# Two transformer blocks in split fp32: every split operand at one place modulo 256 bytes, and block 2's depthwise convolution on VectorE alone

## The chip, the cores and the metric

The kernel runs on one core of one Trainium2 chip. The metric is the device time of one execution in microseconds (us). The engines are called PE (TensorE matmul, with PEld for its weight loads), DVE (VectorE), ACT (ScalarE), POOL (GpSimd) and SP (SyncE, which here issues the loads of the weights).

## The reference

Two different transformer blocks follow each other on one sequence of T = 512 positions and width D = 1024, all in fp32. Cut to what matters here:

```python
def first_block(x, mem, ...):
    h = hybrid_mixer(x, w_in, ...)            # gated recurrence and windowed attention
    x = layer_norm(ALPHA * x + h, ...)
    h = memory_cross_attention(x, mem, xa_wq, xa_wkv, xa_wo)
    x = layer_norm(ALPHA * x + h, ...)
    h = (gelu(g) * val) @ ffn_w_down          # g, val: causal_dwconv(x @ ffn_w_up) in halves
    return layer_norm(ALPHA * x + h, ...)

def second_block(x, ...):
    u = rms_norm(x) @ w_in                    # 1024 -> 2560 columns
    y_a = conformer_conv_mixer(u_conf, ...)
    y_b, y_c, y_d = short_conv_mixer(u_sc), moba_attention(u_att), rglru_mixer(u_lru)
    x = x + rms_norm(concat(y_a, y_b, y_c, y_d) @ w_out)
    return x + rms_norm(square(relu(rms_norm(x) @ mlp_w1)) @ mlp_w2)

def conformer_conv_mixer(u, dw_w, dw_b, gn_g, gn_b):
    val, gate = split(u, 2)                   # 256 channels each
    z = val * sigmoid(gate)
    z = causal_depthwise_conv(z, dw_w) + dw_b # 31 taps for each channel
    return silu(group_norm_channels(z, gn_g, gn_b))
```

## The kernel before

**Split products.** Each fp32 operand of a large product is stored as two fp32r tensors: `split` copies it to the high part on ACT (L107) and subtracts that from the source on DVE to get the low part (L108). One product is then three matmuls: high by high, high by low, low by high. In the channel-major form (`cm_phase`, `cm_mm`, `mm3`, L133 to L135) the weight is stationary and 512 positions of the activations stream past it; a *chunk* is 128 output channels, 8 blocks of k, so 24 matmuls of 512 columns. The first five chunks of a phase (the skew) are done in two halves of 256 columns. In the token-major form (`tm_phase`, L218, L219, L222, and `tm_rotate`) the activations are stationary and 512 columns of the weight stream; a *row* is one block of k for all four token tiles, also 24 matmuls. `tm_cols` (L194 to L196) is a token-major form with 256 or 264 columns.

**Where the operands lie.** The split weights rotate through five buffers each of the tags `wh` and `wl` in the pool `wpool`. A buffer has 1056 floats, 4224 bytes in a partition, which is 16.5 times 256. In the built program the buffers of a tag therefore begin alternately at 224 and 96 modulo 256. The activation sets made by `act_set` (x1 to x4, h1 to h3, and the sets of hidden rows hd, hs, md and ms) all begin at 224 modulo 256, and each block of 512 positions in them is a multiple of 256 bytes. The further weight buffers of a phase's last rows (`extra_pool`: wx2 to wx5) begin at 192 (wx2), 224 (wx3), 96 (wx4) and 224 (wx5).

**Order of the work.** The code is written in program order for each engine, and a scheduler interleaves it; each engine then runs its queue in order. Weights come in 1 MB loads on SP's queue into three raw buffers.

**Block 2's mixer.** After the first five chunks of w_in_2, `taps(c)` for each of the two channel halves c puts the convolution's taps in a list `bg` of pending DVE instructions: one tensor_scalar (L1114) and then scalar_tensor_tensor instructions (L1117) of 128x512, that add one tap each into `cacc`. `NPOOL = (6, 20)` taps of the halves go to POOL at once instead, a product (L1121) and an addition (L1123) each, and `conf_mean` later adds POOL's sum `cacp` to `cacc` (L1130). `pump(RATE)` takes 3 instructions off `bg` after each chunk. Behind the taps come the chunks of the attention's queries and keys; `aq_evac` and `ak_evac` take them out of PSUM into `h3` and `akp`, in halves of 64 partitions, with ACT for the high part (L1051, L1060), DVE for the low part (L1052, L1061), and DVE copies of the key halves to the other 64 partitions (L1063, eight of them). These chunks use three PSUM banks in turn (tag `mm`), so PE starts a chunk only when the one three before it has been taken out. Then four attention heads follow (`at_head`), with the remaining nine chunks between them (`cuts`), the recurrence `lru` after heads 0 and 1, `conf_mean` after head 1 and `conf_norm` after head 2. The product with w_out_2 takes its rows in `order4` = 0, 1 (convolution), 6, 7 (recurrence), 2, 3 (short convolution), 4, 5 (attention); its first pass does two token tiles, 12 matmuls a row.

Of the kernel before, what the change touches and what calls it, by code (L numbers as in the profile page):

```python
# [41 lines left out]
def tile_two_blocks(ctx: ExitStack, tc: tile.TileContext, a: dict, out: bass.AP, dbg=None):  # L42
    nc = tc.nc
    pe, act, dve, pool, sp = nc.tensor, nc.scalar, nc.vector, nc.gpsimd, nc.sync

    def open_pool(name, side="left", space=None, bufs=1):
        kw = {"space": space} if space is not None else {"side": side}
        return tc.alloc_tile_pool(name=name, bufs=bufs, reuse_waits="tile", **kw)
# [9 lines left out]
    wpool = open_pool("wsplit")  # L58
# [47 lines left out]
    def split(hi, lo, src):  # L106
        act.activation(hi, src, AF.Copy)  # L107
        dve.tensor_sub(lo, src, hi.bitcast(F32))  # L108

    def split_w(src, pl=None):  # L110
        shape = list(src.shape)
        n = 1
        for s in shape[1:]:
            n *= s
        if pl is None:
            hi = wpool.tile([P, 1056], F32R, name="wh", tag="wh", bufs=WB)[:, :n]
            lo = wpool.tile([P, 1056], F32R, name="wl", tag="wl", bufs=WB)[:, :n]
        else:
            pl, i = pl
            hi = pl.tile([P, n], F32R, name=f"wxh{i}")  # L120
            lo = pl.tile([P, n], F32R, name=f"wxl{i}")
        if len(shape) == 3:
            hi = hi.rearrange("p (k c) -> p k c", k=shape[1])
            lo = lo.rearrange("p (k c) -> p k c", k=shape[1])
        split(hi, lo, src)
        return hi, lo

    def act_set(pl, name):
        return (pl.tile([P, KC, T], F32R, name=name + "h", tag="ah"),
                pl.tile([P, KC, T], F32R, name=name + "l", tag="al"))  # L130
# [53 lines left out]
    def tm_cols(ws, A, tts, n, psp, tag, bufs, per_bank, evac):  # L184
        for t0 in tts[::per_bank]:
            ps = psp.tile([P, T], F32, name="tmc", tag=tag, bufs=bufs)
            for u in range(per_bank):
                tt = t0 + u
                o = ps[:, u * n:(u + 1) * n]
                for k in range(KC):  # L190
                    wh, wl = ws[k // 4]
                    xh = A[0][:, k, tt * P:(tt + 1) * P]
                    xl = A[1][:, k, tt * P:(tt + 1) * P]
                    pe.matmul(o, xh, wh[:, k % 4, :], start=k == 0, stop=False)  # L194
                    pe.matmul(o, xh, wl[:, k % 4, :], start=False, stop=False)  # L195
                    pe.matmul(o, xl, wh[:, k % 4, :], start=False, stop=k == KC - 1)  # L196
            evac(t0, ps)

    LATE = 4
# [151 lines left out]
    kvg = raw_tile("kvg").rearrange("p (k c) -> p k c", k=KC)  # L351
# [66 lines left out]
    pst = Banks(tr=(3, 4, 5, 6), v=(7,))  # L418
    to_cm(pst, "tr", 4, xr[0][:, 0, :], A0, 0)
    kvg_w = []  # L420
    for k in (0, 4):
        wh = wpool.tile([P, 1056], F32R, name="wh", tag="wh", bufs=WB).rearrange("p (k c) -> p k c", k=4)
        wl = wpool.tile([P, 1056], F32R, name="wl", tag="wl", bufs=WB).rearrange("p (k c) -> p k c", k=4)
        for j in (0, 2):
            split(wh[:, j:j + 2, :], wl[:, j:j + 2, :], kvg[:, k + j:k + j + 2, :])
        kvg_w.append((wh, wl))
    AHEAD = ((1,), (2, 3), (), ())
    for t in range(NT):
        for u in AHEAD[t]:
# [39 lines left out]
    al = xf  # L469
# [285 lines left out]
    lnp = open_pool("ln", side="right")  # L755
# [205 lines left out]
    lnp = open_pool("ln3", side="right")  # L961
# [47 lines left out]
    mx = open_pool("mix2")  # L1009
# [16 lines left out]
    zp = [mx.tile([P, 30 + T], F32, name=f"zp{c}") for c in range(2)]  # L1026
# [29 lines left out]
    def ak_evac(c):  # L1056
        def f(ps):
            for e in range(2):
                (kh, kl), r = ak(2 * c + e), HALF[e]
                act.activation(kh[r, :], ps[r, :], AF.Copy)  # L1060
                dve.tensor_sub(kl[r, :], ps[r, :], kh[r, :].bitcast(F32))  # L1061
                for k in (kh, kl):
                    dve.tensor_copy(k[HALF[1 - e], :], k[r, :].bitcast(F32))  # L1063
        return f

    cs, cx = {}, {}
# [39 lines left out]
    sx = col_blocks(w_in2, 1024, 256)  # L1106
    lg = col_blocks(w_in2, 2304, 256)
    acc = [mx.tile([P, T], F32, name=f"cacc{c}") for c in range(2)]
    accp = [mx.tile([P, T], F32, name=f"cacp{c}") for c in range(2)]
    NPOOL = (6, 20)  # L1110

    def taps(c):
        z, w, n = zp[c], half[:, c, :], NPOOL[c]
        bg.append(lambda: dve.tensor_scalar(acc[c], z[:, 0:T], w[:, 0:1], pv[:, c, DWB:DWB + 1],  # L1114
                                            op0=OP.mult, op1=OP.add))
        for j in range(1, 31 - n):
            bg.append(lambda j=j: dve.scalar_tensor_tensor(acc[c], z[:, j:j + T], w[:, j:j + 1], acc[c],  # L1117
                                                           op0=OP.mult, op1=OP.add))
        for j in range(31 - n, 31):
            dst = accp[c] if j == 31 - n else mx.tile([P, T], F32, name="cact", tag="cact", bufs=1)  # L1120
            pool.tensor_scalar(dst, z[:, j:j + T], w[:, j:j + 1], 0.0, op0=OP.mult, op1=OP.add)  # L1121
            if dst is not accp[c]:
                pool.tensor_add(accp[c], accp[c], dst)  # L1123

    sq, var = {}, {}

    def conf_mean():
        for c in (1, 0):
            if NPOOL[c]:
                dve.tensor_add(acc[c], acc[c], accp[c])  # L1130
            ps = psm.tile([P, T], F32, name="cmu", tag="mm", bufs=3)
            pe.matmul(ps, gmean, acc[c], start=True, stop=True)
            dve.tensor_sub(acc[c], acc[c], ps)
            sq[c] = tmp()
            act.activation(sq[c], acc[c], AF.Square)

    def conf_norm():
        for c in (1, 0):
            var[c] = psm.tile([P, T], F32, name="cva", tag="mm", bufs=3)
            pe.matmul(var[c], gmean, sq[c], start=True, stop=True)  # L1140
        for c in (1, 0):
            act.activation(sq[c], var[c], AF.Ln, bias=eps_t)
        for c in (1, 0):
            act.activation(sq[c], sq[c], AF.Exp, scale=-0.5)
            dve.tensor_mul(acc[c], acc[c], sq[c])
            dve.tensor_scalar(acc[c], acc[c], gnh[:, c, 0:1], gnh[:, c, 1:2], op0=OP.mult, op1=OP.add)
        for c in (1, 0):
            act.activation(sq[c], acc[c], AF.Tanh)
            dve.scalar_tensor_tensor(acc[c], sq[c], 1.0, acc[c], op0=OP.add, op1=OP.mult)
            split(H3[0][:, c, :], H3[1][:, c, :], acc[c])  # L1150
# [74 lines left out]
        act.activation(av[:, t0:t0 + 2, :], ps.rearrange("p (u c) -> p u c", u=2), AF.Copy)  # L1225
        pump(RATE)

    RATE = 3
    ATT = [(aqs[c], aq_evac(c)) for c in range(2)] + [(aks[c], ak_evac(c)) for c in range(2)]
    cm_phase(*MM, ATT, X3, 0, rate=RATE)  # L1230
    tm_block(w_in2, 1792, X3, NT, *MM, av_evac)
# [6 lines left out]
    for c in range(2):  # L1238
        o = psm.tile([P, T], F32, name="ao", tag="o", bufs=1)
        for e in range(2):  # L1240
            h = 2 * c + e
            pts = at_head(h)
            for kb in range(NT):
                pe.matmul(o[64 * e:64 * e + 64, kb * P:], av[:, kb, h * 64:(h + 1) * 64], pts[:, kb, kb * P:],
                          start=kb == 0, stop=kb == NT - 1)
            cm_phase(*MM, rest[cuts[h]:cuts[h + 1]], X3, 0, rate=RATE)
            if h in (0, 1):
                lru(h)
            if h == 1:
# [155 lines left out]
```

## Time and profile before

| what | value |
|---|---|
| median of 3 runs | 1354.44 us (1352.35 to 1355.21) |
| the profiled execution's own time | 1353.82 us |
| its span (first to last instruction) | 1352.1 us |
| PE busy | 1322.2 us, 98% |
| DVE, ACT, POOL busy | 762.1, 531.2, 145.8 us |
| mean granted clock of PE | 0.989 |

The span is what the trace shows; 1.7 us lie outside it. PE's busy time covers nearly all of the span, so a view that only names the busiest engine says little: what counts is how long one matmul takes, and where PE waits or runs at the lower clock.

### The profile page before, as it was taken

The page shows a single profiled execution, that of the slowest core. Times are in us where ns is not written, and L with a number is a line of the kernel's source. Part 1 is how long each engine was busy: PE and PEld are TensorE (multiplying, and loading weights), DVE is VectorE, ACT ScalarE, POOL GpSimd, SP SyncE. Part 2 cuts the span into 40 slices and gives each one's busy share as a digit, 9 for nine tenths or more (in the row PEclk, how much of TensorE's full clock was granted, in tenths as well). Part 3 has the DMA queues.
Part 4 walks back from the last instruction along what each step waited for, and adds up shares of the span by engine and source line. Part 5 has one row for each costly group of instructions (what it writes and reads, how often), then busy time and mean ns, then how long its engine had stood idle before and what let it go on. Part 6 is the DMA issues. An engine that isn't in the chain of part 4 may idle for free.

```text
span 1352.1 us, 17088 instructions
## 1 busy us (share of the span) xinstructions
PE 1322.2 (98%) x6918; PEld 1119.2 (83%) x6918; DVE 762.1 (56%) x1189; ACT 531.2 (39%) x886; POOL 145.8 (11%) x202
## 2 busy tenths in 40 slices
PE   8999999999999999999999997799999999999997
PEld 7898899899889888888888896667898888888886
DVE  5765776665575555566432869986364333532322
ACT  5764564334424333344332332376343223431321
POOL 3220110100010000000000239800100000000000
PEclk9999999998999999999999998899999999999999
DMA  8322354514233323132223121022234332223211
GB/s 259 96 71 64 111 161 163 185 61 157 69 107 121 125 63 125 63 125 94 94 94 125 56 74 63 32 94 91 66 92 127 94 94 94 94 94 109 94 41 53
DMA packets 92148, 134.87 MB, mean 100 GB/s; under 512 B 4572, under 2 KB 77329, under 8 KB 92062
## 3 DMA queue, kind: packets, MB, share of 16 engines
q1 hardware_dynamic: 90030, 129.09, 29.2%
q10 hardware_dynamic: 1384, 2.58, 0.5%
q0 software_dynamic: 656, 2.12, 0.5%
q8 instruction: 54, 0.88, 0.3%
q14 instruction: 24, 0.20, 0.0%
HBM read 131.66 MB, written 2.12 MB: 99 GB/s over the span
## 4 chain that ended last, share of the span: by engine, by line
PE 90%; DVE 7%; ACT 2%; issue 1%; DMA 0%; SPq 0%; DVEq 0%; POOLq 0%; ACTq 0%
PE cm L134 14%; PE cm L135 14%; PE cm L133 14%; PE tm L222 9%; PE tm L219 9%; PE tm L218 9%; DVE cacc L1117 3%; PE tmc L195 2%; PE tmc L196 2%; PE tmc L194 2%; PE tr L289 1%; DVE wl L108 1%; PE tm L133 1%; PE tm L135 1%; PE tm L134 1%
## 5 line engine op out<-in xcount | busy, mean ns | idle before, releaser
L108 DVE TENSOR_TENSOR wl<-rawc,wh 128x1024 fp32r<-128x1024 f32 x140 | 174.8, 1251 | 210.8 <-ACT wh L107 210.3
L107 ACT ACTIVATE wh<-rawc 128x1024 fp32r<-128x1024 f32 x140 | 148.0, 1059 | 228.2 <-PE cm L134 192.4
L108 DVE TENSOR_TENSOR wl<-rawr,wh 128x1024 fp32r<-128x1024 f32 x73 | 88.8, 1222 | 151.6 <-ACT wh L107 151.6
L107 ACT ACTIVATE wh<-rawr 128x1024 fp32r<-128x1024 f32 x73 | 76.9, 1059 | 178.4 <-PE tm L222 129.9
L135 PE MATMUL cm<-x2h,wl 128*128 128x512 f32 (+1 forms) x392 | 146.1, 374 | 0.0
L134 PE MATMUL cm<-x2l,wh 128*128 128x512 f32 (+1 forms) x392 | 145.7, 373 | 0.0
L133 PE MATMUL cm<-x2h,wh 128*128 128x512 f32 (+1 forms) x392 | 143.7, 369 | 0.0
L135 PE MATMUL cm<-x4h,wl 128*128 128x512 f32 (+1 forms) x296 | 107.7, 365 | 0.0
L134 PE MATMUL cm<-x4l,wh 128*128 128x512 f32 (+1 forms) x296 | 107.5, 364 | 0.0
L133 PE MATMUL cm<-x4h,wh 128*128 128x512 f32 (+1 forms) x296 | 106.2, 362 | 0.0
L133 PEld LDWEIGHTS cm<-x2h,wh 128*128 128x128 f32 x392 | 74.2, 190 | 13.9
L134 PEld LDWEIGHTS cm<-x2l,wh 128*128 128x128 f32 x392 | 73.6, 188 | 14.0
L135 PEld LDWEIGHTS cm<-x2h,wl 128*128 128x128 f32 x392 | 73.6, 188 | 12.9
L324 POOL TENSOR_TENSOR rs_r<-rs_e,mhalf 128x1 f32<-128x1 f32 (+1 forms) x16 | 24.3, 1517 | 547.8 <-DVE rs_e L323 547.8
L133 PE MATMUL cm<-x3h,wh 128*128 128x512 f32 (+1 forms) x184 | 65.1, 359 | 4.7 <-DVE h3l L1052 3.8
L617 DVE SCALAR_TENSOR_TENSOR uy<-cm,fw,uy 128x511 f32<-128x511 f32 x88 | 65.5, 746 | 1.4
L134 PE MATMUL cm<-x3l,wh 128*128 128x512 f32 (+1 forms) x184 | 65.2, 356 | 0.0
L135 PE MATMUL cm<-x3h,wl 128*128 128x512 f32 (+1 forms) x184 | 65.0, 355 | 0.0
L133 PEld LDWEIGHTS cm<-x4h,wh 128*128 128x128 f32 x296 | 55.7, 189 | 9.4
L134 PEld LDWEIGHTS cm<-x4l,wh 128*128 128x128 f32 x296 | 55.7, 188 | 9.4
L135 PEld LDWEIGHTS cm<-x4h,wl 128*128 128x128 f32 x296 | 55.7, 188 | 8.9
L194 PE MATMUL tmc<-wh,xh 128*128 128x256 f32 (+1 forms) x160 | 46.7, 292 | 1.2 <-ACT wh L107 1.2
(461 smaller groups left out, 3149.0 us busy)
## 6 DMA issues: line engine op xcount, KB each, us to landing
rawc<-in_ffn_w_up_dram SPq DMA_DIRECT2D x22, 1024.0 KB
rawc<-in_w_in_dram SPq DMA_DIRECT2D x20, 1024.0 KB
rawc<-in_mlp_w_dram SPq DMA_DIRECT2D x16, 1024.0 KB
rawr<-in_mlp_w_dram SPq DMA_DIRECT2D x16, 1024.0 KB
rawr<-in_ffn_w_down_dram SPq DMA_DIRECT2D x11, 1024.0 KB
rawr<-in_w_out_dram SPq DMA_DIRECT2D x10, 1024.0 KB
rawc<-in_xa_wkv_dram SPq DMA_DIRECT2D x8, 1024.0 KB
rawc<-in_xa_wq_dram SPq DMA_DIRECT2D x4, 1024.0 KB
```

Source lines behind the costliest of these rows:

```text
L107: act.activation(hi, src, AF.Copy)
L108: dve.tensor_sub(lo, src, hi.bitcast(F32))
L133: pe.matmul(ps, wh, xh, start=first, stop=False)
L134: pe.matmul(ps, wh, xl, start=False, stop=False)
L135: pe.matmul(ps, wl, xh, start=False, stop=last)
L194: pe.matmul(o, xh, wh[:, k % 4, :], start=k == 0, stop=False)
L195: pe.matmul(o, xh, wl[:, k % 4, :], start=False, stop=False)
L218: pe.matmul(ps[t][h], xh, wh[:, c], start=i == 0, stop=False)
L219: pe.matmul(ps[t][h], xh, wl[:, c], start=False, stop=False)
L222: pe.matmul(ps[t][h], xl, wh[:, c], start=False, stop=i == n - 1)
L617: dve.scalar_tensor_tensor(dst[:, s:], ps[:, :T - s], w[:, j:j + 1], y[:, s:], op0=OP.mult, op1=OP.add)
L1117: bg.append(lambda j=j: dve.scalar_tensor_tensor(acc[c], z[:, j:j + T], w[:, j:j + 1], acc[c], op0=OP.mult, op1=OP.add))
```

## The change

Five edits, in two groups.

The first group is of places. The `wh` and `wl` buffers get 1024 floats (4096 bytes, 16 times 256). The gate, key and value weights of block 1, 2112 floats, no longer fit in two of them, so they are split into three tiles of 3, 3 and 2 blocks of k, and `tm_cols` takes one view for each block. `act_set` allocates 64 floats more for each tensor, and two pads of 56 and 32 floats move the extra weight buffers wx2 and wx4. In the built program the weights, the activation sets and these extra buffers then begin at 224 modulo 256.

The second group is in block 2's mixer. POOL has no taps any more: DVE does all 62 instructions. The eight key copies and the scale and shift of `conf_norm` go from DVE to ACT. `pump` takes 5 instead of 3. `conf_mean` comes after head 2 and `conf_norm` after head 3, and `order4` begins with 6, 7, 2, 3 and ends with 0, 1.

```diff
+    def w_tile(name):
+        return wpool.tile([P, 1024], F32R, name=name, tag=name, bufs=WB)
...
-            hi = wpool.tile([P, 1056], F32R, name="wh", tag="wh", bufs=WB)[:, :n]
-            lo = wpool.tile([P, 1056], F32R, name="wl", tag="wl", bufs=WB)[:, :n]
+            hi = w_tile("wh")[:, :n]
+            lo = w_tile("wl")[:, :n]
...
-    def act_set(pl, name):
-        return (pl.tile([P, KC, T], F32R, name=name + "h", tag="ah"),
-                pl.tile([P, KC, T], F32R, name=name + "l", tag="al"))
+    def act_set(pl, name, shift=0):
+        return tuple(pl.tile([P, KC * T + 64], F32R, name=name + i, tag="a" + i)[:, shift:shift + KC * T]
+                     .rearrange("p (k t) -> p k t", k=KC) for i in "hl")
...
-    for k in (0, 4):
-        wh = wpool.tile([P, 1056], F32R, name="wh", tag="wh", bufs=WB).rearrange("p (k c) -> p k c", k=4)
-        wl = wpool.tile([P, 1056], F32R, name="wl", tag="wl", bufs=WB).rearrange("p (k c) -> p k c", k=4)
-        for j in (0, 2):
-            split(wh[:, j:j + 2, :], wl[:, j:j + 2, :], kvg[:, k + j:k + j + 2, :])
-        kvg_w.append((wh, wl))
+    for k0, k1 in ((0, 3), (3, 6), (6, 8)):
+        wh, wl = [w_tile(n)[:, :(k1 - k0) * 264].rearrange("p (k c) -> p k c", k=k1 - k0) for n in ("wh", "wl")]
+        for j in range(0, k1 - k0, 2):
+            e = min(j + 2, k1 - k0)
+            split(wh[:, j:e, :], wl[:, j:e, :], kvg[:, k0 + j:k0 + e, :])
+        kvg_w += [(wh[:, j, :], wl[:, j, :]) for j in range(k1 - k0)]
...
     lnp = open_pool("ln2", side="right")
+    lnp.tile([P, 56], F32, name="pad")
...
                 for k in (kh, kl):
-                    dve.tensor_copy(k[HALF[1 - e], :], k[r, :].bitcast(F32))
+                    act.activation(k[HALF[1 - e], :], k[r, :].bitcast(F32), AF.Copy)
...
-    NPOOL = (6, 20)
...
-        for j in range(1, 31 - n):
+        for j in range(1, 31):
             bg.append(lambda j=j: dve.scalar_tensor_tensor(acc[c], z[:, j:j + T], w[:, j:j + 1], acc[c],
                                                            op0=OP.mult, op1=OP.add))
-        for j in range(31 - n, 31):
-            dst = accp[c] if j == 31 - n else mx.tile([P, T], F32, name="cact", tag="cact", bufs=1)
-            pool.tensor_scalar(dst, z[:, j:j + T], w[:, j:j + 1], 0.0, op0=OP.mult, op1=OP.add)
-            if dst is not accp[c]:
-                pool.tensor_add(accp[c], accp[c], dst)
...
-            if NPOOL[c]:
-                dve.tensor_add(acc[c], acc[c], accp[c])
...
-            dve.tensor_scalar(acc[c], acc[c], gnh[:, c, 0:1], gnh[:, c, 1:2], op0=OP.mult, op1=OP.add)
+            act.activation(acc[c], acc[c], AF.Identity, scale=gnh[:, c, 0:1], bias=gnh[:, c, 1:2])
...
-    RATE = 3
+    RATE = 5
...
-            if h == 1:
+            if h == 2:
                 pump(len(bg))
                 conf_mean()
-            if h == 2:
+            if h == 3:
                 conf_norm()
...
     lnp = open_pool("ln4", side="right")
+    lnp.tile([P, 32], F32, name="pad")
...
-    order4 = [0, 1, 6, 7, 2, 3, 4, 5]
+    order4 = [6, 7, 2, 3, 4, 5, 0, 1]
```

How the order of the instructions moves is seen at three places. The first is DVE's queue in block 2's mixer while the second key chunk is taken out of PSUM, before the change (the two `cacc` are the convolution's two halves, `zp` its padded input, `h3h`, `h3l` and `akp` the places of the keys):

```order
L1117 SCALAR_TENSOR_TENSOR cacc_6826<-zp_6820,half,cacc_6826 128x512
L1061 TENSOR_TENSOR h3l<-cm,h3h 64x512
L1063 CAST h3h<-h3h 64x512
L1117 SCALAR_TENSOR_TENSOR cacc_6825<-zp_6819,half,cacc_6825 128x512
L1117 SCALAR_TENSOR_TENSOR cacc_6826<-zp_6820,half,cacc_6826 128x512
L1063 CAST h3l<-h3l 64x512
L108 TENSOR_TENSOR wl<-rawc,wh 128x1024
L1117 SCALAR_TENSOR_TENSOR cacc_6825<-zp_6819,half,cacc_6825 128x512
L1061 TENSOR_TENSOR akp<-cm,akp 64x512
L1063 CAST akp<-akp 64x512
L1061 TENSOR_TENSOR h3l<-cm,h3h 64x512
L1063 CAST h3h<-h3h 64x512
```

The same place in DVE's queue after the change (L1123 is the tap, L1069 the low part of the keys, L113 the low part of a weight):

```order
L1123 SCALAR_TENSOR_TENSOR cacc_6831<-zp_6825,half,cacc_6831 128x512
L1069 TENSOR_TENSOR h3l<-cm,h3h 64x512
L1123 SCALAR_TENSOR_TENSOR cacc_6830<-zp_6824,half,cacc_6830 128x512
L1123 SCALAR_TENSOR_TENSOR cacc_6831<-zp_6825,half,cacc_6831 128x512
L1123 SCALAR_TENSOR_TENSOR cacc_6830<-zp_6824,half,cacc_6830 128x512
L113 TENSOR_TENSOR wl<-rawc,wh 128x1024
L1123 SCALAR_TENSOR_TENSOR cacc_6831<-zp_6825,half,cacc_6831 128x512
L1069 TENSOR_TENSOR akp<-cm,akp 64x512
L1123 SCALAR_TENSOR_TENSOR cacc_6830<-zp_6824,half,cacc_6830 128x512
L1069 TENSOR_TENSOR h3l<-cm,h3h 64x512
L1123 SCALAR_TENSOR_TENSOR cacc_6831<-zp_6825,half,cacc_6831 128x512
L1123 SCALAR_TENSOR_TENSOR cacc_6830<-zp_6824,half,cacc_6830 128x512
```

The copies have left the queue, and more taps stand between the evacuations. Counted over the stage, 24 taps stand ahead of the first softmax row in DVE's queue before and 27 after; behind it 10 before and 33 after.

The second place is ACT's queue over the same chunks, before the change:

```order
L107 ACTIVATE wh<-rawc 128x1024
L1060 ACTIVATE h3h<-cm 64x512
L107 ACTIVATE wh<-rawc 128x1024
L1060 ACTIVATE akp<-cm 64x512
L1060 ACTIVATE h3h<-cm 64x512
L1060 ACTIVATE akp<-cm 64x512
L1225 ACTIVATE av<-tmc 128x512
```

And after it (L1068 is the high part of the keys, L1071 the copies, L112 the high part of a weight, L1224 the values):

```order
L1068 ACTIVATE h3h<-cm 64x512
L1071 ACTIVATE h3h<-h3h 64x512
L112 ACTIVATE wh<-rawc 128x1024
L1068 ACTIVATE akp<-cm 64x512
L1071 ACTIVATE h3l<-h3l 64x512
L1068 ACTIVATE h3h<-cm 64x512
L1071 ACTIVATE akp<-akp 64x512
L1071 ACTIVATE h3h<-h3h 64x512
L1071 ACTIVATE akp<-akp 64x512
L1068 ACTIVATE akp<-cm 64x512
L1224 ACTIVATE av<-tmc 128x512
```

ACT now has the copies between the high parts; a copy of a low part waits there for DVE's subtraction.

The third place is the convolution's norm on DVE, before the change (`conf_norm` ends in the two splits `h3l<-cacc`; `aL` is a softmax row, of head 3):

```order
L1145 TENSOR_TENSOR cacc_6826<-cacc_6826,tmp 128x512
L1186 ISA aL,ast<-as,ab 128x256
L1186 ISA ast 128x1
L1145 TENSOR_TENSOR cacc_6825<-cacc_6825,tmp 128x512
L1189 RECIPROCAL ast<-ast 128x1
L1146 TENSOR_SCALAR cacc_6826<-cacc_6826,gnh 128x512
L108 TENSOR_TENSOR h3l<-tmp,h3h 128x512
...
L1149 SCALAR_TENSOR_TENSOR cacc_6825<-tmp,cacc_6825 128x512
L108 TENSOR_TENSOR h3l<-cacc_6826,h3h 128x512
L108 TENSOR_TENSOR h3l<-cacc_6825,h3h 128x512
```

And after it:

```order
L113 TENSOR_TENSOR h3l<-tmp,h3h 128x512
L1144 TENSOR_TENSOR cacc_6831<-cacc_6831,tmp 128x512
L1144 TENSOR_TENSOR cacc_6830<-cacc_6830,tmp 128x512
L1148 SCALAR_TENSOR_TENSOR cacc_6831<-tmp,cacc_6831 128x512
L1148 SCALAR_TENSOR_TENSOR cacc_6830<-tmp,cacc_6830 128x512
L113 TENSOR_TENSOR h3l<-cacc_6831,h3h 128x512
L113 TENSOR_TENSOR h3l<-cacc_6830,h3h 128x512
L113 TENSOR_TENSOR h3l<-ao,h3h 128x512
L113 TENSOR_TENSOR wxl_8192<-rawr,wxh_8191 128x1024
```

The norm has moved from among head 3's softmax rows to behind the last of them, next to the last split of the attention's output and the first extra weights of w_out_2. The rows of PE's and SP's queues keep their order here, but for the two products with `gmean` and the order of w_out_2's rows.

## Rows read from the trace of the kernel before

**Rows 1.** The page: PE's busy time, and the chain by line.

```profile
PE 1322.2 (98%) x6918; PEld 1119.2 (83%) x6918; DVE 762.1 (56%) x1189; ACT 531.2 (39%) x886; POOL 145.8 (11%) x202
PE cm L134 14%; PE cm L135 14%; PE cm L133 14%; PE tm L222 9%; PE tm L219 9%; PE tm L218 9%; DVE cacc L1117 3%; PE tmc L195 2%; PE tmc L196 2%; PE tmc L194 2%; PE tr L289 1%; DVE wl L108 1%; PE tm L133 1%; PE tm L135 1%; PE tm L134 1%
```

**Rows 2.** Three windows: length, busy PE, PEld, DVE, ACT, POOL; PE clock, DMA.

```profile
800.00:840.00 40.00, 33.46 (x157) 28.04 (x157) 39.71 (x34) 10.74 (x14) 36.60 (x26) 0.88 0.32 105
840.00:880.00 40.00, 30.11 (x157) 25.79 (x156) 39.53 (x51) 13.27 (x22) 31.77 (x25) 0.86 0.08 27
880.00:925.00 45.00, 44.15 (x183) 30.00 (x182) 34.48 (x77) 37.00 (x59) 0.00 (x0) 1.00 0.27 94
```

**Rows 3.** Waits in block 2's mixer: us in total, times, longest.

```profile
ACT h3l L1051 <- DVE h3h L1052: 16.7, 2, 8.9
PE tmc L194 <- DVE h3l L1061: 4.9, 1, 4.9
```

**Rows 4.** PE's timeline (start, us), first matmuls of chunks of mlp_w1.

```profile
1004.57 0.28 PE L133 MATMUL cm<-x4h,wh 128*128 128x256 f32 x1
1007.30 0.28 PE L133 MATMUL cm<-x4h,wh 128*128 128x256 f32 x1
...
1034.74 0.39 PE L133 MATMUL cm<-x4h,wh 128*128 128x512 f32 x1
1040.19 0.39 PE L133 MATMUL cm<-x4h,wh 128*128 128x512 f32 x1
1045.74 0.40 PE L133 MATMUL cm<-x4h,wh 128*128 128x512 f32 x1
...
1062.47 0.39 PE L133 MATMUL cm<-x4h,wh 128*128 128x512 f32 x1
```

**Rows 5.** PE's timeline, first matmuls of two chunks of ffn_w_up, 35 chunks apart.

```profile
438.50 0.39 PE L133 MATMUL cm<-x2h,wh 128*128 128x512 f32 x1
...
633.57 0.39 PE L133 MATMUL cm<-x2h,wh 128*128 128x512 f32 x1
```

**Rows 6.** PE's timeline, first matmuls of rows of mlp_w2.

```profile
1201.07 0.39 PE L218 MATMUL tm<-wh,mdh 128*128 128x512 f32 x1
...
1206.53 0.39 PE L218 MATMUL tm<-wh,mdh 128*128 128x512 f32 x1
...
1228.69 0.39 PE L218 MATMUL tm<-wh,ms0h 128*128 128x512 f32 x1
```

**Rows 7.** DVE's groups by form in 789 to 945: busy us, mean ns.

```profile
L1117 DVE SCALAR_TENSOR_TENSOR cacc<-zp,half,cacc 128x512 f32<-128x512 f32 x34 | 42.5, 1276 | 0.2
L108 DVE TENSOR_TENSOR wl<-rawc,wh 128x1024 fp32r<-128x1024 f32 x15 | 22.5, 1498 | 5.1 <-ACT wh L107 5.0
L108 DVE TENSOR_TENSOR wl<-rawr,wh 128x1024 fp32r<-128x1024 f32 x5 | 6.0, 1220 | 0.2 <-ACT wh L107 0.2
L1063 DVE CAST akp<-akp 64x512 fp32r<-64x512 f32 x4 | 4.4, 1106 | 0.1
...
L1063 DVE CAST h3h<-h3h 64x512 fp32r<-64x512 f32 x2 | 2.1, 1058 | 0.1
...
L1130 DVE TENSOR_TENSOR cacc<-cacc,cacp 128x512 f32<-128x512 f32 x2 | 1.4, 682 | 0.0
...
L1063 DVE CAST h3l<-h3l 64x512 fp32r<-64x512 f32 x2 | 1.2, 611 | 0.0
```

**Rows 8.** Timelines of POOL (its last tap) and of DVE (a tap behind it).

```profile
872.38 1.57 POOL L1123 TENSOR_TENSOR cacp<-cacp,cact 128x512 f32<-128x512 f32 x1
...
874.17 0.73 DVE L1117 SCALAR_TENSOR_TENSOR cacc<-zp,half,cacc 128x512 f32<-128x512 f32 x1
874.82 1.21 DVE L108 TENSOR_TENSOR wl<-rawc,wh 128x1024 fp32r<-128x1024 f32 x1
```

**Rows 9.** Timelines of the norm's last instructions and of PE reaching w_out_2.

```profile
928.68 1.29 DVE L108 TENSOR_TENSOR h3l<-cacc,h3h 128x512 fp32r<-128x512 f32 x2 [0.57 <-ACT h3h L107]
...
938.96 0.40 PE L218 MATMUL tm<-wh,h3h 128*128 128x512 f32 x1
```

More of the change, by code (lines that the diff above doesn't have):

```diff
@@ L190, in tm_cols @@
                 for k in range(KC):
-                    wh, wl = ws[k // 4]
+                    wh, wl = ws[k]
                     xh = A[0][:, k, tt * P:(tt + 1) * P]
                     xl = A[1][:, k, tt * P:(tt + 1) * P]
-                    pe.matmul(o, xh, wh[:, k % 4, :], start=k == 0, stop=False)
-                    pe.matmul(o, xh, wl[:, k % 4, :], start=False, stop=False)
-                    pe.matmul(o, xl, wh[:, k % 4, :], start=False, stop=k == KC - 1)
+                    pe.matmul(o, xh, wh, start=k == 0, stop=False)
+                    pe.matmul(o, xh, wl, start=False, stop=False)
+                    pe.matmul(o, xl, wh, start=False, stop=k == KC - 1)
             evac(t0, ps)
@@ L607, in tm_block @@
         v = load_cols(w, c0, 256)
-        tm_cols([split_w(v[:, 0:4, :]), split_w(v[:, 4:8, :])], A, range(tt_n), 256, psp, tag, bufs, 2, evac)
+        ws = [split_w(v[:, k:k + 4, :]) for k in (0, 4)]
+        tm_cols([(ws[k // 4][0][:, k % 4, :], ws[k // 4][1][:, k % 4, :]) for k in range(KC)], A, range(tt_n), 256,
+                psp, tag, bufs, 2, evac)
     qk = {}
@@ L1108, in tile_two_blocks @@
     acc = [mx.tile([P, T], F32, name=f"cacc{c}") for c in range(2)]
-    accp = [mx.tile([P, T], F32, name=f"cacp{c}") for c in range(2)]
-    NPOOL = (6, 20)
     def taps(c):
-        z, w, n = zp[c], half[:, c, :], NPOOL[c]
+        z, w = zp[c], half[:, c, :]
         bg.append(lambda: dve.tensor_scalar(acc[c], z[:, 0:T], w[:, 0:1], pv[:, c, DWB:DWB + 1],
                                             op0=OP.mult, op1=OP.add))
-        for j in range(1, 31 - n):
+        for j in range(1, 31):
             bg.append(lambda j=j: dve.scalar_tensor_tensor(acc[c], z[:, j:j + T], w[:, j:j + 1], acc[c],
                                                            op0=OP.mult, op1=OP.add))
-        for j in range(31 - n, 31):
-            dst = accp[c] if j == 31 - n else mx.tile([P, T], F32, name="cact", tag="cact", bufs=1)
-            pool.tensor_scalar(dst, z[:, j:j + T], w[:, j:j + 1], 0.0, op0=OP.mult, op1=OP.add)
-            if dst is not accp[c]:
-                pool.tensor_add(accp[c], accp[c], dst)
     sq, var = {}, {}
```

## The prediction

> **What bounds the kernel now.** I read the page first, then windows over the span, then single stretches. The page has PE busy for 98% of the span, and of the lines on the chain that ended last, the only one above 1% that isn't PE's is DVE's with the convolution's taps, 3% [rows 1]. So there are two places to look for time: the length of a matmul where PE never stops, and the stage where it does stop.
>
> The stage where it stops is block 2's mixer. [...] In the window from 880 to 925 POOL is done, PE is busy for 44.15 of 45 us at clock 1.00, and DVE is idle for 10.5 us [rows 2]. What PE lost is 6.54 + 9.89 + 0.85 = 17.3 us of idle time, and 0.12 x 40 + 0.14 x 40 = 10.4 us of clock, 27.7 us in all. This is the cap on what any relief of DVE can give. The waits say which way the loss goes: ACT waits 8.9 us at a time for DVE's half of the evacuation of the queries, and PE 4.9 us for that of the keys [rows 3], because the three PSUM banks are freed only by evacuations that are queued behind taps in DVE's queue.
>
> Where PE never stops, equal chunks don't take equal time. In mlp_w1 (x4 at 224 modulo 256) the chunk whose high and low weights both lie at 224 takes 1040.19 - 1034.74 = 5.45 us; the next, with one of the two at 96, 5.55; and a cycle of five chunks, which goes through all combinations, 27.73, so 5.546 each [rows 4]. The halves of a chunk with 256 columns show none of it: 2.73 us [rows 4], half of 5.45. In ffn_w_up the mean over 35 chunks is (633.57 - 438.50) / 35 = 5.573 [rows 5]. In mlp_w2 the row with all at 224 takes 1206.53 - 1201.07 = 5.46, and the cycle of five (1228.69 - 1201.07) / 5 = 5.524 [rows 6]. So a matmul of 512 columns is slower by some 2% when its streamed operand, its stationary one or the next weight load don't lie at the same place modulo 256.
>
> **Term 1, places.** After the change all three lie at 224 in nearly every matmul of 512 columns. I price the chunks at 5.45 and the rows at 5.46, which this trace shows for that placing:
> - ffn_w_up: 44 chunks less 5 of the skew, 39 x (5.573 - 5.45) = 4.8 us;
> - mlp_w1: 27 x (5.546 - 5.45) = 2.6;
> - 15 more channel-major chunks of block 1, taken like ffn_w_up's: 1.8;
> - mlp_w2: 32 rows x (5.524 - 5.46) = 2.0;
> - ffn_w_down's 22 rows and the 24 of the three 1024-wide output products, taken like mlp_w2's: 46 x 0.064 = 2.9.
>
> Sum 14.1 us. Upper bound 15.2, by ffn_w_up's gap for mlp_w1 also (+0.7) and some 0.4 of rounding; lower bound 10.3, with 0.096 for all 81 chunks (7.8) and half the gap for the 78 rows (2.5), since one row alone carries 5.46. The 13 mixer chunks are left to term 2. Everything with 256 columns counts as nothing, by the half chunks [rows 4]. The split into three tiles at the front takes one more pair of short splits and a fifth buffer's turn; it stands at nothing, with up to 2 us either way inside the range.
>
> **Term 2, the mixer.** I count what leaves DVE's queue, since DVE sets the pace there.
> - Taps: 34 now cost 42.5 us, 1.276 each, with POOL working on the same inputs beside them [rows 7]. The one that runs behind POOL's last instruction is followed after 874.82 - 874.17 = 0.65 us [rows 8]. 60 x 0.65 = 39.0, so 26 more taps cost 3.5 us *less*. If the price is that row's full 0.73, it is 43.8, or 1.3 more.
> - Eight key copies go: 4.4 + 2.1 + 1.2 = 7.7 us less [rows 7]. ACT gets them; nothing hides them but ACT's own idle time, and ACT is busy for 10.74 + 13.27 of these 80 us [rows 2].
> - The two additions of POOL's sum go: 1.4 us less [rows 7].
> - Fifteen low parts of weights cost 1.498 us each in this stage against 1.220 for the same size later [rows 7]: 4.2 us less if that too is POOL's doing, nothing if not.
>
> Sum: -3.5 - 7.7 - 1.4 - 4.2 = -16.8 us of DVE work, in a stage where DVE is never idle. Its least is -7.7 - 1.4 + 1.3 = -7.8 us; its most is the cap, -27.7, when PE never waits and never drops its clock. Between them I take 16.8. The larger rate of 5 puts 27 taps ahead of the first softmax row instead of 24 (27 x 0.65 = 17.6 us against 24 x 1.276 = 30.6), so the queries and keys come out earlier; behind it 33 stand instead of 10, 21.5 us against 12.8, and of these 8.7 us more the 10.5 us that DVE is idle from 880 to 925 can hold most [rows 2]. That is why I go neither below the ledger nor to the cap.
>
> **The moved norm.** It costs nothing as long as PE has other rows of w_out_2. Before, its last splits end at 928.68 + 1.29 = 929.97, and PE reaches w_out_2 at 938.96 [rows 9]. After, it stands behind head 3, and rows 6, 7, 2, 3, 4, 5 come first: six rows of 12 matmuls, 6 x 5.46 / 2 = 16 us of cover [rows 6]. What is queued behind it on DVE are the attention's last split and the extra weights; these would be late next. Without cover the loss is about the time from the norm's start to its last split: up to 10 us. I set it at nothing.
>
> **Sum.** 1353.82 - 14.1 - 16.8 = **1322.9 us**. The profiled execution lies 0.6 us below the median of the runs shown, which is inside their scatter.
>
> **The rivals.**
> - *Places don't matter* (B): the difference of 2% would come from something that goes along with the buffers' turn, and the kernel would end at 1353.82 - 16.8 = 1337.0 us. For it: the trace has no stretch in which every chunk lies at 224, only single ones. Against it: the pattern follows the turn in mlp_w1 and mlp_w2 alike, and vanishes with 256 columns [rows 4, 6]. [...]
> - *DVE stays the pace-setter in the later heads* (C): the 33 taps behind the first softmax row hold the softmax rows of heads 1 and 2 up, PE waits there as it did before 880, and the mixer gives its least: 1353.82 - 14.1 - 7.8 = 1331.9 us. For it: a queue that runs in order and five taps after each chunk; against it: 10.5 us of DVE's idle time in just that stretch [rows 2].
> - *The cap is reached* (E): 1353.82 - 14.1 - 27.7 = 1312.0 us. For it: PE was at clock 1.00 with 98% as soon as POOL had ended [rows 2].
> - *The taps' length isn't POOL's doing* (D), the slower side: they keep 1.276 us, since one row alone shows the shorter price. Then 60 x 1.276 - 42.5 = +34.1, less 7.7 and 1.4 is +25.0, and the time is 1353.82 - 14.1 + 25.0 = 1364.7 us. It decides from 60 p = 42.5 + 9.1 + 14.1, a price of p = 1.095 us. Against it: the weights' low parts are longer too while POOL works [rows 7].
>
> **How the numbers follow.** Forecast 0.58, C 0.20, B 0.09, E 0.08, D 0.05. The range goes from 1311 (E, with the upper bound of term 1) to 1337 (B, and C with the lower bound of term 1 at 1335.7); outside it are D, half of B and the tails of E, less than 2 in 10. A measurement of this kernel can tell about 0.2%, 2.7 us, from no change. Every case but D ends faster by more than that; of D I give 0.01 to no change, for a tap price near 1.095: faster 0.95, same 0.01, slower 0.04. The forecast's own range is 1316 to 1330.
>
> **What the changed profile would show.** Term 1: chunks of ffn_w_up and mlp_w1 all at 5.45 us, rows of mlp_w2 and ffn_w_down at 5.46, with no turn of five. Term 2: taps at 0.65 to 0.73 us, low parts of weights at 1.22 in the mixer, DVE less than full from 800 to 880, the clock there nearer 1.00, ACT's wait for the query's evacuation down from 8.9 us. The norm: no wait of PE for the convolution's h3 in w_out_2. The prediction is wrong if chunks at one place still take 5.55, if taps stay near 1.28 us with POOL silent, or if PE's idle time has only moved to the heads after 860.

## The result and the profile after

The changed kernel takes 1322.18 us (median of 4 runs, 1320.57 to 1322.66) against 1354.69 us; the ratio is 0.9761, with a 95% interval from 0.9744 to 0.9778. That is 32.5 us less. The profiled execution has a span of 1320.6 us against 1352.1.

The first view is again the page, PE's busy time and the chain by line. DVE's taps have gone from 3% of the chain to 1% [rows 1]:

```profile
PE 1300.4 (98%) x6918; PEld 1114.9 (84%) x6918; DVE 744.3 (56%) x1204; ACT 534.2 (40%) x895; POOL 76.1 (6%) x152
PE cm L139 15%; PE cm L138 15%; PE cm L140 15%; PE tm L224 9%; PE tm L223 9%; PE tm L227 9%; PE tmc L200 2%; PE tmc L201 2%; PE tmc L199 2%; PE tr L294 1%; PE tm L140 1%; PE tm L139 1%; PE tm L138 1%; PE num L680 1%; DVE cacc L1123 1%; PE mls L660 1%
```

To see where the time went, one lays the same points of PE's program beside each other. PE's timeline of the kernel before, at the first matmul of six stages (the seventh is w_out_2 in [rows 9]; the columns are start and duration in us):

```profile
63.37 0.40 PE L133 MATMUL swop<-swpth,swv 128*128 128x512 f32 x1
...
432.95 0.40 PE L133 MATMUL cm<-x2h,wh 128*128 128x512 f32 x1
...
650.27 0.40 PE L218 MATMUL tm<-wh,hdh 128*128 128x512 f32 x1
...
804.48 0.39 PE L133 MATMUL cm<-x3h,wh 128*128 128x512 f32 x1
...
1018.03 0.39 PE L133 MATMUL cm<-x4h,wh 128*128 128x512 f32 x1
...
1167.83 0.40 PE L218 MATMUL tm<-wh,mdh 128*128 128x512 f32 x1
```

PE's timeline of the changed kernel at the same points, and between them at a few first matmuls of chunks and rows:

```profile
65.31 0.39 PE L138 MATMUL swop<-swpth,swv 128*128 128x512 f32 x1
...
433.33 0.40 PE L138 MATMUL cm<-x2h,wh 128*128 128x512 f32 x1
...
640.08 0.39 PE L138 MATMUL cm<-x2h,wh 128*128 128x512 f32 x1
...
645.52 0.39 PE L223 MATMUL tm<-wh,hdh 128*128 128x512 f32 x1
...
798.15 0.40 PE L138 MATMUL cm<-x3h,wh 128*128 128x512 f32 x1
...
911.84 0.48 PE L223 MATMUL tm<-wh,h3h 128*128 128x512 f32 x1
...
928.99 0.39 PE L223 MATMUL tm<-wxh,h3h 128*128 128x512 f32 x1
...
991.89 0.40 PE L138 MATMUL cm<-x4h,wh 128*128 128x512 f32 x1
...
1008.24 0.39 PE L138 MATMUL cm<-x4h,wh 128*128 128x512 f32 x1
...
1013.68 0.39 PE L138 MATMUL cm<-x4h,wh 128*128 128x512 f32 x1
...
1138.80 0.39 PE L223 MATMUL tm<-wh,mdh 128*128 128x512 f32 x1
...
1160.56 0.39 PE L223 MATMUL tm<-wh,mdh 128*128 128x512 f32 x1
...
1166.00 0.39 PE L223 MATMUL tm<-wh,mdh 128*128 128x512 f32 x1
```

The differences of these starts give the account of the 31.5 us of span:

| stretch of PE's program | change, us |
|---|---|
| start to the window attention of block 1 | +1.9 |
| on to ffn_w_up | -1.6 |
| ffn_w_up | -5.1 |
| ffn_w_down, to block 2's first full chunk | -1.6 |
| mixer of block 2 | -20.8 |
| w_out_2 and the skewed start of mlp_w1 | +1.0 |
| mlp_w1 | -2.9 |
| mlp_w2 to the end | -2.5 |

A chunk of mlp_w1 now takes 1013.68 - 1008.24 = 5.44 us, a chunk of ffn_w_up (640.08 - 433.33) / 38 = 5.44, a row of mlp_w2 1166.00 - 1160.56 = 5.44 [rows 4 to 6].

The mixer's windows in the changed kernel, with the columns of [rows 2]: PE is full up to 840, POOL is silent, and what is left of the old loss is 4.70 us of idle time and 0.04 x 40 = 1.6 us of clock, 6.3 us where there were 27.7 from 800 to 925 [rows 2]. DVE is hardly less full than before: 39.23 and 38.41 of 40 us, after 39.71 and 39.53.

```profile
800.00:840.00 40.00, 40.00 (x227) 35.14 (x226) 39.23 (x63) 21.17 (x32) 0.00 (x0) 1.00 0.31 104
840.00:880.00 40.00, 35.30 (x144) 24.82 (x143) 38.41 (x77) 25.79 (x43) 0.00 (x0) 0.96 0.22 79
880.00:925.00 45.00, 45.00 (x201) 33.98 (x200) 29.50 (x57) 28.32 (x47) 0.00 (x0) 1.00 0.22 71
```

The waits there (us in total, times, longest): ACT's wait for the queries is down from 8.9 us at a time to 2.8 [rows 3], and PE waits for softmax rows on DVE.

```profile
ACT h3l L1059 <- DVE h3h L1060: 5.1, 2, 2.8
...
PE apt L1192 <- DVE aL L1189: 2.3, 1, 2.3
...
PE ao L1243 <- DVE apts L1193: 1.3, 1, 1.3
```

DVE's groups from 789 to 925 (busy us, mean ns): 60 taps now take what 34 took, and fifteen low parts of weights take 18.3 us instead of 22.5 [rows 7].

```profile
L1123 DVE SCALAR_TENSOR_TENSOR cacc<-zp,half,cacc 128x512 f32<-128x512 f32 x60 | 42.7, 744 | 0.2
L113 DVE TENSOR_TENSOR wl<-rawc,wh 128x1024 fp32r<-128x1024 f32 x15 | 18.3, 1219 | 5.2 <-ACT wh L112 5.1
```

### The profile page after: what moved, and what is told of

The parts are those of the page before. It is cut to its first block, busy times and chain, and to the rows that moved or that the text cites. A ratio compares the mean times of both kernels' runs of the same rounds, so it can differ in the third digit from the quotient of the medians.

```text
span 1320.6 us, 17065 instructions
## 1 busy us (share of the span) xinstructions
PE 1300.4 (98%) x6918; PEld 1114.9 (84%) x6918; DVE 744.3 (56%) x1204; ACT 534.2 (40%) x895; POOL 76.1 (6%) x152
## 4 chain that ended last, share of the span: by engine, by line
PE 94%; DVE 3%; ACT 2%; issue 0%; DMA 0%; POOL 0%; SPq 0%; DVEq 0%; POOLq 0%; ACTq 0%
PE cm L139 15%; PE cm L138 15%; PE cm L140 15%; PE tm L224 9%; PE tm L223 9%; PE tm L227 9%; PE tmc L200 2%; PE tmc L201 2%; PE tmc L199 2%; PE tr L294 1%; PE tm L140 1%; PE tm L139 1%; PE tm L138 1%; PE num L680 1%; DVE cacc L1123 1%; PE mls L660 1%
## 5 line engine op out<-in xcount | busy, mean ns | idle before, releaser
L113 DVE TENSOR_TENSOR wl<-rawc,wh 128x1024 fp32r<-128x1024 f32 x140 | 170.7, 1222 | 203.6 <-ACT wh L112 203.3
L112 ACT ACTIVATE wh<-rawc 128x1024 fp32r<-128x1024 f32 x140 | 147.7, 1059 | 222.0 <-PE cm L139 190.8
L113 DVE TENSOR_TENSOR wl<-rawr,wh 128x1024 fp32r<-128x1024 f32 x73 | 88.9, 1223 | 147.4 <-ACT wh L112 147.4
L112 ACT ACTIVATE wh<-rawr 128x1024 fp32r<-128x1024 f32 x73 | 76.9, 1060 | 175.3 <-PE tm L227 126.6
```

## The experiments

Times are medians; the ratio is to the kernel before on the same chip, with its interval. The changed kernel's is 0.9761.

### Each half of the change alone

The first run is the kernel before with the first group of edits, the second that with the second group; together they are the diff above.

> The kernel before with the first group of edits alone (1024-float weight buffers, three tiles for the gate, key and value weights, longer activation sets, two pads); mixer, rate, norm and order of rows as before. Theory (places decide the length of a 512-column matmul): in the changed kernel's trace PE has gained 6.5 us by the start of block 2's mixer and 5.4 us from mlp_w1 to the end, so about 12 us in all and some 1342 us; chunks of mlp_w1 at 5.45 us. Rival (what shortened these stages is not the places): 1354 us, chunks still in a cycle of 5.45 to 5.6.

> The kernel before with the second group of edits alone (all taps on VectorE, key copies and scale on ScalarE, rate 5, later norm, order of rows); buffers and places as before. Theory (the mixer's gain is DVE's, independent of places): PE gained 20.8 us between 804 and 939 in the changed kernel, about 1.5 us of it from places, so 19 us and some 1335 us; taps at 0.74 us. Rival (part of the mixer's gain came from the places, since PE waits less with shorter chunks): over 1340 us. Sum of the two parts against the whole change: equal within 3 us if they are independent.

The places alone gave 1339.14 us, 0.9884 [0.9868, 0.9900], or 16.0 us; the mixer alone 1334.74 us, 0.9851 [0.9835, 0.9867], or 20.4 us. The sum, 36.4 us, is 3.9 us more than the whole change gave, where 3 were expected at most; each interval is some 2 us wide to either side. The profiles show what most of the excess is. Their spans are 13.2 us (places) and 20.1 us (mixer) shorter than before, but 2.6 of the 20.1 lie between window attention and ffn_w_up, where none of the mixer's edits is: that profile lacks a drop of PE's clock which those of before and of the whole change (0.84 in each from 310 to 332), and that of places alone, have (last section). Without these 2.6 us the two make 30.7 us, against 31.5 for the whole, and no overlap is left. In the stretch of the mixer PE gains 19.3 us by the mixer's edits alone and 1.4 by the places alone, together 20.7 of the table's 20.8.

With places alone the taps still take 1276 ns, and with the mixer alone 743: the taps' price has nothing to do with places. Both theories held, both rivals fell.

### Is it the place, and modulo what?

The changed kernel with its activation sets shifted by 32 floats; the second run has 64 in the same place.

```diff
-    def act_set(pl, name, shift=0):
+    def act_set(pl, name, shift=32):
```

> The changed kernel with one number altered: every activation set begins 128 bytes later in its tile, at 96 modulo 256, while the weights stay at 224. Sizes, order and work are the same. Theory (same place modulo 256 is what counts): no 512-column product with weights has its operands at one place any more; chunks 5.55 to 5.6 us instead of 5.45, rows 5.52 to 5.6 instead of 5.46, so 12 to 22 us more, 1334 to 1344 us. Rival (the size or the turn of the weight buffers counts, not the place against the activations): no change, 1322 us.

> The changed kernel with every activation set 256 bytes later, again at 224 modulo 256 but at another place modulo 512 and above. Theory (only the place modulo 256 counts): no change, 1322 us within 2 us. Rival (places modulo 512 or more count as well): between 1322 and the time of the shift by 128 bytes.

A shift of 128 bytes gave 1340.32 us, 0.9896 [0.9880, 0.9912]; one of 256 bytes 1320.50 us, 0.9747 [0.9730, 0.9764]. PE's timelines of mlp_w1 show the whole of it. With the activations at 96 modulo 256 and the weights at 224, one chunk to the next:

```profile
1006.55 0.39 PE L138 MATMUL cm<-x4h,wh 128*128 128x512 f32 x1
...
1012.12 0.40 PE L138 MATMUL cm<-x4h,wh 128*128 128x512 f32 x1
```

With both at 224, but 256 bytes further:

```profile
1001.09 0.39 PE L138 MATMUL cm<-x4h,wh 128*128 128x512 f32 x1
...
1006.53 0.39 PE L138 MATMUL cm<-x4h,wh 128*128 128x512 f32 x1
```

That is 5.57 against 5.44 us for the same 24 matmuls, with the same sizes, the same turn of buffers and the same order. A chunk was 2.4% longer with streamed and stationary operand 128 bytes apart modulo 256. Of other distances the traces have one, 32 bytes: the matmuls with wx2 at 192 started 233 ns apart on average before, and 227 with wx2 at 224 after. The rival in the prediction would have left both runs alike.

### GpSimd or the schedule?

The changed kernel with GpSimd's products and sums as before:

```diff
+    NPOOL = (6, 20)
...
-        for j in range(1, 31):
+        for j in range(1, 31 - n):
...
+        for j in range(31 - n, 31):
+            dst = accp[c] if j == 31 - n else mx.tile([P, T], F32, name="cact", tag="cact", bufs=1)
+            pool.tensor_scalar(dst, z[:, j:j + T], w[:, j:j + 1], 0.0, op0=OP.mult, op1=OP.add)
+            if dst is not accp[c]:
+                pool.tensor_add(accp[c], accp[c], dst)
...
+            dve.tensor_add(acc[c], acc[c], accp[c])
```

> The changed kernel with 26 of the 60 taps given back to GpSimd (6 and 20, as before) and its sum added by VectorE; all else as in the change, rate 5 and the key copies on ScalarE included. Theory (GpSimd's work beside it is what makes VectorE's two-input instructions long): the 34 taps go back to about 1.28 us and the weights' low parts to 1.5, VectorE's work in the stage grows by about 42.5 + 1.4 + 4.2 - 42.7 = 5 us, and the time by 2 to 10 us, to 1324 to 1332 us. Rival (the taps were long for another reason): taps stay at 0.74 us, VectorE has 26 of them less, and the time is 1322 us or below.

The time was 1337.39 us, 0.9881 [0.9856, 0.9905], 15.2 us more than the changed kernel and beyond the expected 10. DVE's groups of that run:

```profile
L1125 DVE SCALAR_TENSOR_TENSOR cacc<-zp,half,cacc 128x512 f32<-128x512 f32 x34 | 43.5, 1307 | 0.2
L113 DVE TENSOR_TENSOR wl<-rawc,wh 128x1024 fp32r<-128x1024 f32 x15 | 22.6, 1509 | 6.4 <-ACT wh L112 6.4
```

So with 26 taps fewer on DVE the taps, the low parts and the whole are slower: the direction of the theory, and by medians three quarters of the mixer's gain. By the starts in PE's timelines it is nearly all: from block 2's first full chunk to mlp_w1 PE gained 19.8 us in the changed kernel, 2.6 in this run, and 2.1 with places alone.

The next run leaves all taps on DVE and adds only the loop with `dst` of the diff above, so that GpSimd does its old 26 products and 24 sums beside them and nothing reads `accp`. The one after has GpSimd only write zeros, in place of that loop:

```diff
+        for _ in range((40, 160)[c]):
+            pool.memset(accp[c], 0.0)
```

> The changed kernel, all 62 instructions of the convolution on VectorE, and beside them GpSimd doing the 26 products and 24 sums that it did before, whose result nothing uses. Theory (GpSimd reading SBUF is what lengthens VectorE's two-input instructions): while GpSimd runs, taps take about 1.28 us instead of 0.74, some 68 us of GpSimd's work slow VectorE by up to 25 us, and the time is 1335 to 1350 us. Rival (the number of GpSimd's taps that VectorE has to wait for or the schedule was the cause): 1322 us.

> The changed kernel with GpSimd filling two unused 128x512 tiles with zeros 200 times beside the convolution, writes without a read. [...] Rival (any access of GpSimd to SBUF slows VectorE): taps over 0.9 us and 1330 us or more.

Idle reads: 1345.22 us, 0.9939 [0.9924, 0.9955], 23 us more for work that no one waits for; the mean tap is 1117 ns, although GpSimd ends at 870 us and the last tap at 901.

```profile
L1124 DVE SCALAR_TENSOR_TENSOR cacc<-zp,half,cacc 128x512 f32<-128x512 f32 x60 | 65.2, 1117 | 0.2
```

Idle writes: 1338.58 us, 0.9877 [0.9861, 0.9893]. The time is that of the rival, but its reason is not: the taps are at 740 ns and the low parts of the weights at 1214, untouched by 102 us of writing. In DVE's groups the loss is in another, of two instructions:

```profile
L1124 DVE SCALAR_TENSOR_TENSOR cacc<-zp,half,cacc 128x512 f32<-128x512 f32 x60 | 42.5, 740 | 0.2
...
L1121 DVE TENSOR_SCALAR cacc<-zp,half,pv 128x512 f32<-128x512 f32 x2 | 16.4, 8180 | 0.0
```

And DVE's timeline has one of the two, the first instruction of a convolution half, standing for 15.64 us; the other took 0.71 us:

```profile
794.68 15.64 DVE L1121 TENSOR_SCALAR cacc<-zp,half,pv 128x512 f32<-128x512 f32 x1
...
814.43 0.71 DVE L1121 TENSOR_SCALAR cacc<-zp,half,pv 128x512 f32<-128x512 f32 x1
```

GpSimd writes beside both, but not alike. Beside the first it is busy for all of 15 us; around the second it leaves small gaps and is busy for 3.65 of 4 (columns as in [rows 2]):

```profile
795.00:810.00 15.00, 15.00 (x85) 13.14 (x85) 15.00 (x1) 4.24 (x5) 15.00 (x33) 1.00 0.20 67
812.00:816.00 4.00, 4.00 (x20) 3.24 (x19) 4.00 (x7) 0.00 (x0) 3.65 (x7) 1.00 0.10 18
```

Beside GpSimd's products and sums, which read and write, a tap took 1276 ns on average in the kernel before, 1307 with GpSimd's taps back and 1117 in the run of idle reads, whose last taps come after GpSimd's end; beside writes alone it took 740, as long as without GpSimd (744). The tensor_scalar took 15.64 us beside unbroken writes and 0.71 beside writes with gaps. Why it stood for so long, no run here shows.

### The small edits of the mixer

```diff
-                    act.activation(k[HALF[1 - e], :], k[r, :].bitcast(F32), AF.Copy)
+                    dve.tensor_copy(k[HALF[1 - e], :], k[r, :].bitcast(F32))
```

> The changed kernel with the eight key copies back on VectorE. Theory (VectorE's ledger): with GpSimd silent a copy costs about 0.6 us, so 5 us more in a stage in which VectorE is busy for 39 of 40 us; PE loses 2 to 5 us, 1324 to 1327 us. Rival (in this stage PE is the bound, which was busy for all of 800 to 840): within 1 us of 1322.

1320.92 us, 0.9752 [0.9731, 0.9773]: no difference clear of the scatter, so the theory of the ledger fell. The group of copies shows why the forecast of 7.7 us was not theirs: without GpSimd a copy takes 422 ns, not 1106 [rows 7].

```profile
L1071 DVE CAST akp<-akp 64x512 fp32r<-64x512 f32 x4 | 1.7, 422 | 0.1
```

```diff
-            if h == 2:
+            if h == 1:
                 pump(len(bg))
                 conf_mean()
-            if h == 3:
+            if h == 2:
                 conf_norm()
...
-    order4 = [6, 7, 2, 3, 4, 5, 0, 1]
+    order4 = [0, 1, 6, 7, 2, 3, 4, 5]
```

> The changed kernel with the convolution's mean and norm one head earlier again (after heads 1 and 2) and the old order of w_out_2's rows. Theory (the later norm is what makes room for 60 taps): at the end of head 1 some 12 taps are still pending and go out at once, 12 x 0.66 = 8 us in front of head 2's softmax rows; PE loses 3 to 8 us, 1325 to 1330 us. Rival (the norm's place costs nothing, as it was forecast for the later one): within 1.5 us of 1322.

1322.16 us, 0.9759 [0.9741, 0.9777]: the norm's place is worth nothing either way, and the theory that it makes room for the taps fell. In PE's timeline of this run the mixer gains 18.9 us instead of 20.8, and the next stretch gains 0.7 where the changed kernel lost 1.0: the norm's place only moves these 1.7 to 1.9 us from one stretch to the other.

```diff
-    RATE = 5
+    RATE = 3
```

> The changed kernel with 3 taps taken off the list after each chunk instead of 5. Theory A (the taps among heads 0 and 1 are what PE waits for between 850 and 865, 4.7 us idle and 1.7 us of clock): with fewer of them there the waits go, 3 to 6 us less, 1316 to 1319 us. Theory B (the 20 or more taps left for head 2 then go out at once, 13 to 17 us in one piece, and hold up head 3's softmax): 2 to 8 us more, 1324 to 1330 us.

1319.82 us, 0.9740 [0.9721, 0.9760], and it tests neither theory: DVE's instructions come in the same order, row for row, as with a rate of 5. Where a tap stands is the scheduler's choice; between 3 and 5 the rate sets nothing. Read as a repeat of the changed kernel, the run shows that medians scatter by some 2 us.

### What PE still loses

To move taps for certain, these two runs give the first half a dependence on an attention head. The second has `h == 1` in the line that is added, and `pump`, `conf_mean` and `conf_norm` all at `h == 3`.

```diff
-    for c in (1, 0):
-        taps(c)
+    taps(1)
...
             pts = at_head(h)
+            if h == 0:
+                dve.tensor_copy(acc[0][:, 0:1], pts[:, NT - 1, T - 1:T])
+                taps(0)
```

> The changed kernel with the taps of the first channel half made to depend on head 0's weights (one extra one-column copy into its accumulator), so that the scheduler can't put them earlier: 29 taps still stand ahead of the first softmax row, but 41 instead of 62 ahead of head 2's, 55 ahead of the last. Theory A (the taps among heads 0 and 1 cause PE's 4.7 us of idle time and 1.7 us of clock between 840 and 880): 3 to 6 us less, 1316 to 1319 us. Theory B (the waits there are a chain of softmax, transposes and recurrence that taps don't lengthen): within 1.5 us of 1322.

> As the run with half 0 after head 0, but the taps of the first half wait for head 1, and mean and norm both come after head 3: no tap stands between the softmax rows of heads 0 and 1. Theory A: 4 to 6.4 us less than the changed kernel, unless the norm's chain, now with both its steps behind head 3, outlasts the 16 us of w_out_2's other rows; then PE waits for h3 there and the gain is given back (1318 to 1328 us). Theory B: no change in the heads, and only the possible loss at w_out_2.

1328.34 us, 0.9797 [0.9780, 0.9814], and 1334.49 us, 0.9846 [0.9830, 0.9862]: 6 and 12 us slower than the changed kernel, where Theory A had 3 to 6 us less for the first and, with the gain given back, up to 1328 us for the second. Yet Theory A is right about the place. In the second run's window PE no longer stops at all (its profile is of a run of 1329.97 us, under its median):

```profile
840.00:880.00 40.00, 40.00 (x181) 29.90 (x180) 34.04 (x75) 28.80 (x51) 0.00 (x0) 1.00 0.23 80
```

PE's timeline then shows where it was given back. It reaches the extra weights of w_out_2 only at 938.66, 9.67 us *later* than the changed kernel (928.99), and after a wait of 5.17 us; a longer wait follows at the transposes before mlp_w1, for DVE's sum of squares `ssv` of a token tile. The changed kernel has neither; its one wait from 895 to 1000 is 1.3 us.

```profile
938.66 3.78 PE L223 MATMUL tm<-wxh,h3h 128*128 128x512 f32 x8 [5.17 <-ACT wxh L112]
...
965.83 1.94 PE L294 MATMUL tr<-ident,hx 128*128 128x128 f32 x8 [6.89 <-DVE ssv L980]
```

ACT's timeline has the split of the extra weights, the three `wxh`, behind the last step of the norm:

```profile
936.17 0.63 ACT L112 ACTIVATE h3h<-cacc 128x512 fp32r<-128x512 f32 x1 [1.37 <-DVE cacc L1148]
937.55 2.95 ACT L112 ACTIVATE wxh<-rawr 128x1024 fp32r<-128x1024 f32 x3 [0.76 <-DVE h3l L113]
```

The norm is late because its half of the taps is. The 16 us of cover did not hold for a convolution that ends this late. The first run's PE, too, gains in the heads (37.84 of 40 us busy from 840 to 880), and loses most of that again up to 925 (42.96 of 45, where the changed kernel has 45.00). Its 6 us lie behind, at the same transposes: a wait of 3.95 us, and 7 us at half the clock (0.51) right after it. What makes `ssv` late in these runs was not followed.

```profile
962.84 1.06 PE L294 MATMUL tr<-ident,hx 128*128 128x128 f32 x8 [3.95 <-DVE ssv L980]
...
964.00:971.00 7.00, 6.61 (x28) 6.25 (x29) 4.73 (x8) 3.07 (x10) 1.08 (x2) 0.51 0.00 0
```

(The second line is a window, with the columns of [rows 2].)

## Why the prediction was right

The forecast was 1322.9 us, the result 1322.18. The parts are less exact than the sum, so that it fits to 1 us is partly luck.

- **Places: right, mechanism and size.** Forecast 14.1 us; the stretches that consist mostly of such matmuls gained 1.6 + 5.1 + 1.6 + 2.9 + 2.5 = 13.7. The run with places alone gained 16.0 by its median; in its profile the same stretches have 13.6, and the one with w_out_2, which the forecast counts too, 0.7. The price of 5.45 and 5.46, read from one chunk and one row at the right place, came out as 5.44 everywhere.
- **The mixer: right in its mechanism, 3 to 4 us too small.** Forecast 16.8 from DVE's ledger; PE gained 20.8, of which 1.4 are the places' by the run with places alone; with w_out_2's stretch, into which the norm moves, it is 19.8. The ledger took the *busy* 1.276 us for the old taps and 0.65, the time to the next start, for the new ones; by busy time the taps' sum did not move at all (42.5 to 42.7 us). The weights' low parts came out as priced, 4.2 us less. What it missed on the other side is that the loss was of PE's waits and clock, not of DVE's hours: once the queries and keys came out in time, PE went from 27.7 us lost to 6.3, while DVE stayed as good as full. The sign "DVE less than full" therefore hardly came. The measured 20.8 lies between the ledger and the cap, 4.0 above the one and 6.9 below the other.
- **The key copies: a wrong attribution.** Their 7.7 us were in the sum as what the move to ACT gives. The move gives nothing: back on DVE, the copies leave the time as it is. It was GpSimd's work beside them that made the longest of them 1106 ns instead of 422.
- **The rate: a wrong reason.** The prediction named the larger rate for the 27 taps ahead of the first softmax row. The order doesn't depend on it.
- **Costs set at nothing.** The norm was one, rightly. The front was not quite nothing: it lost 1.9 us, which stood in the range as 2, and shows only in the profiles with the new weight tiles there (with the mixer's edits alone that stretch is 0.2 us longer). The stretch from w_out_2 to mlp_w1 lost 1.0 us, which with the norm early is a gain of 0.7, made up for in the mixer. These 2.9 us and the 4 us too few in the mixer all but cancel each other.
- **The rivals.** Of C the place was right (PE waits for softmax rows behind taps among heads 0 and 1), but the 6.3 us are all that is left there, and the mixer did not fall to its least of 7.8. E fell with these 6.3 us. D fell with taps at 744 ns, B with the shift by 128 bytes.

## What to carry to other kernels

Before giving GpSimd a part of VectorE's work, look at what VectorE's two-input instructions cost while it runs: here, with 26 taps moved away, the 34 others were 1.7 times as long (1276 against 744 ns), and taking them back added nothing to DVE's time in taps (42.5 and 42.7 us). Where PE is full, read the starts of equal chunks of matmuls side by side; a turn of lengths that follows the turn of buffers can be a place effect, which a shift of one operand tests; here buffers of a multiple of 256 bytes, with the other operand at the same place, removed it (a chunk of ffn_w_up went from 5.573 us on average to 5.44). Don't credit an edit with time that another edit of the same change gives back: the copies, the rate and the norm's place looked like parts of the gain and were none.

## What was not expected of the hardware

One tensor_scalar stood for 15.64 us, the length of some thirty of GpSimd's writes of 0.53 us, beside a stream that left the taps at 740 ns and the low parts of the weights at 1214; that run was 16.4 us slower, 15.1 of them in the mixer by PE's starts, about as much as with 26 taps back on GpSimd (15.2).

PE's clock also drops in some profiles, and not in others, in block 1's cross attention. The windows of this stretch in the changed kernel and in the run with the key copies on VectorE (columns as in [rows 2]):

```profile
310.00:332.00 22.00, 22.00 (x148) 20.25 (x147) 11.08 (x30) 9.94 (x26) 0.00 (x0) 0.84 0.44 148
```

```profile
310.00:332.00 22.00, 22.00 (x161) 19.70 (x160) 13.90 (x34) 11.28 (x28) 0.00 (x0) 1.00 0.53 191
```

PE is busy throughout in both, yet the first is at a mean granted clock of 0.84 (1.00 from 310 to 318, 0.50 from 320 to 324, 1.00 again from 326 on), and gets through 13 matmuls fewer. In both, PE has run 32 matmuls of 4 columns just before, in 2.14 us in the first; the clock falls behind them in the first and not in the second, and no run shows why. By PE's starts, 368.0 us from window attention to ffn_w_up against 365.2, it is worth 2.8 us, and is likely a good part of the scatter between runs of one kernel, though only one run of each was profiled; it is also why small effects were read from the starts of stretches and not from medians.
